# A hybrid encoder trunk: where in memory the two operands of the 256-column products lie to each other

## The chip, the core and the metric

The kernel runs on one NeuronCore of a Trainium2 chip. The metric is the device time of one execution in microseconds (us), median of several runs. The engines are TensorE (PE in the profile; its weight loads are shown apart as PEld), VectorE (DVE), ScalarE (ACT), GpSimd (POOL) and SyncE (SP, which issues most DMAs). A product here is one instruction of TensorE: 128 rows of *moving* data, 128 to 512 columns wide, stream past 128 x 128 *stationary* data, which a weight load has put into the array before.

## The reference

Two layers over 256 tokens of 2048 channels, all float32. Cut to what is computed:

```python
for layer in range(2):
    h = rms_norm(x, norm_mixer_g[layer])
    if layer % 2 == 0:      # convolution module
        a, gate = split(h @ w_pw1 + b_pw1)            # 2048 -> 2 x 2048
        u = a * sigmoid(gate)
        u = depthwise_causal_conv(u, w_dw, width=31) + b_dw
        x = x + silu(layer_norm(u, ln_g, ln_b)) @ w_pw2 + b_pw2
    else:                   # multi-head latent attention, 16 heads, chunk mask
        c_q, c_kv, k_pe = split(h @ w_in, [512, 1024])
        q = rms_norm(c_q, q_norm_g) @ w_q_up          # per head 128 + 64 (rotary)
        kv = rms_norm(c_kv, kv_norm_g) @ w_kv_up      # per head keys 128, values 128
        x = x + attention(q, kv, k_pe) @ w_o
    h = rms_norm(x, norm_mlp_g[layer])
    x = x + square(relu(h @ w1)) @ w2                 # 2048 -> 8192 -> 2048
return rms_norm(x, final_norm_g)
```

## The kernel before

**Products in parts.** To come near float32, every operand is split into a high part, which ScalarE writes as a rounded copy (`hi`, type float32r), and a low part, which VectorE (in the convolution mostly GpSimd) writes as the rest (`lo`). A product of two matrices is then three products of TensorE: high x high, high x low, low x high. `mm3` (L194 to L198) issues the three with the tokens or weights' parts as its caller orders them.

**Stages.** In order of time: the convolution's first product (L858 to L860, about 19 to 208 us) with the depthwise taps on VectorE (L960) under it; layer norm and the second product (L196 to L198, moving weights 512 wide); the first MLP (about 320 to 1010 us); the attention (its input product to 1040 us, queries, keys, values and scores to about 1150, the output product behind); the second MLP.

**The tokens.** The normalised input of a stage lies in four tiles `xt`, which `open_xt` (L316) takes from a pool at the right end of the memory: for each of 16 pieces of 128 channels the high part (256 columns, one for each token) and right behind it the low part. `xh(k)` is a piece's high part, `xl(k)` its low part, `xhl(k)` both in one operand of 512 columns. Before the change one set of `xt` serves the convolution and the first MLP and the attention's input product; a second one is opened for the second MLP.

**The MLP's first product.** Weights w1 come in units of 128 output columns, each in two chunks of 8 pieces. `hi_lo` (L418) makes the two tiles of a chunk; the low tile is longer by `LO_GAP` = 64 floats, and its data begin `at` floats behind its start. In `up_unit` the high weights are stationary against `xhl(k)`, 512 columns (L515), and the low weights against `xh(k)`, 256 columns (L513). A unit's order on TensorE is 8 products of L515, 16 of L513, 8 of L515. MLP units of the second product (512 columns, L196 to L198) stand between them.

**The convolution's first product.** Here the weights are stationary and the tokens move: for each block of 128 channels (16 blocks) there are 16 pieces x 2 halves (value and gate) x 3 products = 96 products of 256 columns: high weights against `xh(k)` (L858) and `xl(k)` (L859), low weights against `xh(k)` (L860). VectorE does most of the 31 taps of each block, into banks of sums which ScalarE starts (L916).

**The attention's products.** Keys (L1420 to L1422) and queries (L1443 to L1445) have weights stationary and the normalised compressed tokens `kvh`, `kvl`, `qh`, `ql` moving, 256 columns. Values and the queries' rotary parts (`mm3`, L196 to L198) have it the other way round: tokens stationary, weights moving, 256 columns. The scores' rotary part (L1525) has `kpA` moving and `qpA` stationary.

**Where things lie.** Pads of a few floats (`PAD_CONST`, `PAD_RIGHT`, `PAD_O` and so on) shift the tiles behind them. *Distance* means in this document: start address of a product's moving operand minus that of its stationary operand, in bytes within a partition, modulo 256. It is worked out from the addresses that the built program gives its tiles. Consecutive pieces lie a multiple of 256 bytes apart, so the distance to the next product's stationary data is the same inside a run of like products.

Of the kernel before, what the change touches and what calls it, by code (L numbers as in the profile page):

```python
# [10 lines left out]
F32 = mybir.dt.float32  # L11
# [7 lines left out]
P = 128  # L19
# [19 lines left out]
PAD_SMALL = 8  # L39
PAD_RIGHT = 40  # L40
LO_GAP = 64
PAD_STATS = 48
PAD_O = 64
WB = 6
LOOK = WB // 2 - 1
LAST_PE = 22
# [37 lines left out]
def trunk_kernel(  # L84
# [55 lines left out]
    def nm(s):  # L140
        uid[0] += 1
        return f"{s}_{uid[0]}"
# [104 lines left out]
    def to_T(src, k0, hi, lo, gain, pt=None):  # L247

        pt = pt if pt is not None else tr_tile()
        for j in range(2):  # L250
            for t in range(T):
                nc.tensor.transpose(  # L252
                    pt[:, j * S + t * P : j * S + (t + 1) * P],
                    src[:, t, (k0 + j) * P : (k0 + j + 1) * P],
                    ident,
                )
        ps = [pt[:, j * S : (j + 1) * S] for j in range(2)]
        for j in range(2):
            hi_part(ps[j], hi(k0 + j), gain[:, k0 + j : k0 + j + 1])
        for j in range(2):  # L260
            lo_part(ps[j], hi(k0 + j), lo(k0 + j), gain[:, k0 + j : k0 + j + 1])
# [46 lines left out]
    def right_pool(name, bufs):  # L308

        xt_cx[0].close()  # L310
        xt_cx[0] = ExitStack()
        return xt_cx[0].enter_context(tc.tile_pool(name=name, bufs=bufs, side="right", reuse_waits="tile"))

    ctx.callback(lambda: xt_cx[0].close())

    def open_xt(name):  # L316
        pool = right_pool(name, 1)
        xt[:] = [
            pool.tile([P, KC // NNB, 2 * S], F32R, name=nm("xt")) for _ in range(NNB)
        ]  # L320

    xhl = lambda k: xt[k // 4][:, k % 4, :]
    xh = lambda k: xhl(k)[:, :S]
    xl = lambda k: xhl(k)[:, S:]
    open_xt("xt0")
    spare = []

    xh_kt = lambda k, t: xh(k)[:, t * P : (t + 1) * P]
# [2 lines left out]
    def residual_stage(last, gain, r_scale=None):  # L331


        ssq = small.tile([P, T, NNB], F32, tag="ssq", name=nm("ssq"), bufs=2) if last else None

        def add(n, ps, t):
            sl = slice(n * NB, (n + 1) * NB)
            if r_scale is None:
                nc.vector.tensor_tensor(xs[:, t, sl], ps[t], xs[:, t, sl], op=ALU.add)
            else:  # L340
                nc.vector.scalar_tensor_tensor(
                    out=xs[:, t, sl], in0=ps[t], scalar=r_scale[:, t : t + 1], in1=xs[:, t, sl],
                    op0=ALU.mult, op1=ALU.add,
                )

        def prepare(n, only=None):
            sl = slice(n * NB, (n + 1) * NB)
            if last:
                if gain is not None:
                    for j in range(2):  # L350
                        to_T(xs, 4 * n + 2 * j, xh, xl, gain)
                for t in range(T) if only is None else [only]:
                    nc.scalar.activation(spare[-1](), xs[:, t, sl], AF.Square, accum_out=ssq[:, t, n : n + 1])

        return ssq, add, prepare
# [63 lines left out]
    def hi_lo(n, at=0):  # L419
        hi = wpool.tile([P, n, NB], F32R, tag="hi", name=nm("hi"), bufs=WB)  # L420
        lo = wpool.tile([P, n * NB + LO_GAP], F32R, tag="lo", name=nm("lo"), bufs=WB)
        return [hi, lo[:, at : at + n * NB].rearrange("p (a b) -> p a b", b=NB)]

    def split_into(parts, src):
        nc.scalar.activation(parts[0], src, AF.Copy)  # L425
        nc.vector.tensor_tensor(parts[1], src, parts[0].bitcast(F32), op=ALU.subtract)  # L426
# [52 lines left out]
    def mlp(layer, ssq, next_gain, finish=None, before=None, last_w1=None):  # L479
# [11 lines left out]
        def up_units(hs, q, p, extra):  # L491

            sevens = SEVENS[layer][q]
            held = {}
            large = p in sevens or (q == PARTS - 1 and p in LATE_G[layer])

            def up_unit(b):
                ps = []

                def chunk(h):  # L500
                    def prep(raw, parts):
                        parts[h] = [a.rearrange("p a (j n) -> p (a j) n", n=P) for a in hi_lo(2, LO_GAP - 8)]
                        split_into(parts[h], raw[:, 8 * h : 8 * h + 8, :])

                    def run(parts):
                        if not ps:
                            ps.append(acc_tile())
                        wh, wl = parts.pop(h)
                        for low in (h, 1 - h):
                            for j in range(8):  # L510
                                k = 8 * h + j
                                if low:
                                    nc.tensor.matmul(ps[0][:, :S], wl[:, j, :], xh(k), start=False, stop=False)  # L513
                                else:
                                    nc.tensor.matmul(ps[0], wh[:, j, :], xhl(k), start=k == 0, stop=k == KC - 1)  # L515

                    def out():
                        if b == 0:
                            held["u"] = u_tile()
                        nc.scalar.activation(held["u"][:, b, :], ps[0], AF.Copy)  # L520

                    if h == 0:
                        return Chunk(prep, run)
                    return Chunk(prep, run, [add, lambda: None, square, forms, part] + extra if b == 1 else [], now=out)

                unit = Unit(rows(w1, 0, KC, ((q * NPAIR + p) * 2 + b) * P, P), KC, [chunk(h) for h in range(2)])
                unit.last_read = 1
                return unit

            def add():  # L530
                v = held["u"][:, :, :S]
                nc.vector.tensor_tensor(v, v, held["u"][:, :, S:], op=ALU.add)

            def square():
                n_s[0] += large
                v = held["u"][:, :, :S]
                nc.scalar.activation(v, v, AF.Relu)
                if p in sevens:
                    held["f"] = f = f_tile()
                    nc.scalar.activation(f[:, 0:4, :].rearrange("p (b t) n -> p b (t n)", b=2), v, AF.Square)  # L540
                    held["src"], shape, tag, n = f[:, 1:8, :], [P, 7, P], "s", N_S
                else:
                    nc.scalar.activation(v, v, AF.Square)
                    held["src"], shape = v, [P, 2, S]
                    tag, n = ("s", N_S) if large else ("g", N_G)
                held["hl"] = [mp.tile(shape, F32R, tag=tag + c, name=nm(tag + c), bufs=n) for c in "hl"]

            def forms():
                if p in sevens:
                    f = held["f"]  # L550
                    nc.vector.tensor_tensor(
                        f[:, 4:6, :], f[:, 0:1, :].broadcast_to([P, 2, P]), f[:, 1:3, :], op=ALU.subtract
                    )
                    nc.vector.tensor_tensor(f[:, 6, :], f[:, 1, :], f[:, 5, :], op=ALU.subtract)
                    nc.vector.tensor_tensor(f[:, 7, :], f[:, 3, :], f[:, 6, :], op=ALU.subtract)

            def part():
                hs[p] = held["hl"]
                split_into(hs[p], held["src"])

            if large:
                blocked[square] = lambda: n_s[0] < N_S and not (p in sevens and sums_left)
            return [up_unit(b) for b in range(2)]
# [235 lines left out]
    with ExitStack() as cx:  # L799
# [21 lines left out]
        sl_ = cv.tile([P, KC, S], F32R, name="sl_")  # L821
        cv.tile([P, PAD_STATS], F32, name="pad_stats")
        stats = cv.tile([P, T, KC // 2, 6], F32, name="stats")
# [201 lines left out]
        with tc.manual_schedule():  # L1025
# [57 lines left out]
            for c in range(1, KC + 1):  # L1083
                n = UC * c
# [84 lines left out]
            for m in range(NP):  # L1169
# [17 lines left out]
                sl = slice(i * NB, (i + 1) * NB)  # L1187
                nc.vector.tensor_tensor(xs[:, t, sl], xs[:, t, sl], b2[:, sl], op=ALU.add)

        ssq, add, prepare = residual_stage(True, g_mlp[0])  # L1190
        for b in range(2):
            for t in range(T):
# [62 lines left out]
    with ExitStack() as cx:  # L1255
        at = cx.enter_context(tc.tile_pool(name="at", bufs=1, reuse_waits="tile"))
# [58 lines left out]
        raws, parts = {}, {}  # L1315
# [28 lines left out]
        def prefetch(n=9):  # L1344
            while pending and n > 0:
# [3 lines left out]
                if h == 1:  # L1349
                    u_load(u + 3)  # L1350

        kvh = at.tile([P, KR // P, S], F32R, name="kvh")
        kvl = at.tile([P, KR // P, S], F32R, name="kvl")
        qh = at.tile([P, QR // P, S], F32R, name="qh")
# [15 lines left out]
        for i in range(2):  # L1370
            for j in range(HG):
                nc.scalar.activation(qpB[i][DR:, j, :], mq[DR:, :], AF.Copy)
        pad_o = at.tile([P, PAD_O], F32, name="pad_o")
        nc.gpsimd.memset(pad_o, 0.0)
# [202 lines left out]
        with tc.manual_schedule():  # L1577
# [9 lines left out]
            for k in range(KC):  # L1587
                u, j = divmod(k, 2)
# [17 lines left out]
            for k in range(KC):  # L1606
                u, j = divmod(k, 4)
# [59 lines left out]
            for g in range(NG):  # L1667
                for i in range(HG):
                    h = g * HG + i

                    n = -(-len(work) // (HG - i))
# [116 lines left out]
```

## Time and profile before

| | |
|---|---|
| Median of 3 runs | 1936.2 us (1936.07 to 1936.22) |
| Profiled execution | 1935.74 us, its span 1933.9 us |
| TensorE's granted clock, mean | 0.999 |
| HBM | 363.68 MB read, 189 GB/s over the span |

The page's groups name a line, an engine, an operation, the tiles (out<-in), the shapes, how many there are, then their busy time in us, the mean duration of one in ns, and idle time of the engine before them. The timeline has start and duration in us. A product's duration (about 0.28 us for 256 columns, 0.39 for 512) is longer than its spacing to the next one, since products overlap in the pipeline; the spacing is read from the starts.

### The profile page before, as it was taken

The numbers are of one execution on the slowest core, as the hardware profiler recorded it, in microseconds if no ns is written. First come the engines' busy times: TensorE is split into PE (matmuls) and PEld (weight loads), VectorE is DVE, ScalarE is ACT, GpSimd is POOL, SyncE is SP. The second block draws the span as 40 slices with busy tenths as digits, with TensorE's granted clock in tenths as the row PEclk, the third lists the DMA queues.
The fourth block names the chain that finished last, engine by engine and source line by source line (L and its number), as shares of the span: only waits on it lengthen the run. The fifth ranks groups of instructions, "written<-read, shape, count | busy, mean of one in ns | idle before, by whom it ended". The sixth has DMA issues, their size and how long they took to land.

```text
span 1933.9 us, 28479 instructions
## 1 busy us (share of the span) xinstructions
PE 1910.2 (99%) x10778; PEld 1676.2 (87%) x10778; DVE 1651.6 (85%) x2374; ACT 1204.9 (62%) x1709; POOL 224.0 (12%) x183
## 2 busy tenths in 40 slices
PE   7999999999999999999999999999999999999998
PEld 7999888888888888888899998888888888888886
DVE  5999875789999999999976665657999999999887
ACT  5556664766666666666566665556766666666654
POOL 5999400000000000000001410000000000000000
PEclk9999999999999999999999999999999999999999
DMA  8666456857666667666646445765667766766663
GB/s 235 185 176 176 141 186 174 220 172 208 197 207 204 205 199 212 202 198 215 198 143 181 123 152 175 198 184 174 203 190 210 214 196 195 214 202 197 211 222 109
DMA packets 407113, 367.62 MB, mean 190 GB/s; under 512 B 15416, under 2 KB 351936, under 8 KB 406720
## 3 DMA queue, kind: packets, MB, share of 16 engines
q1 hardware_dynamic: 405952, 363.63, 63.0%
q10 hardware_dynamic: 1024, 2.17, 0.3%
q8 instruction: 84, 1.38, 0.3%
q14 instruction: 53, 0.43, 0.1%
HBM read 363.68 MB, written 2.10 MB: 189 GB/s over the span
## 4 chain that ended last, share of the span: by engine, by line
PE 98%; DVE 1%; DMA 1%; ACT 0%; issue 0%; DVEq 0%; ACTq 0%
PE acc L515 24%; PE acc L196 15%; PE acc L197 15%; PE acc L198 15%; PE acc L513 12%; PE acc L859 3%; PE acc L858 3%; PE acc L860 3%; PE acc L252 1%; PE sum L908 1%; PE acc L1443 0%; PE acc L1445 0%; PE acc L1444 0%; PE acc L1420 0%; PE acc L1421 0%; PE acc L1422 0%
## 5 line engine op out<-in xcount | busy, mean ns | idle before, releaser
L426 DVE TENSOR_TENSOR lo<-raw,hi 128x1024 fp32r<-128x1024 f32 (+1 forms) x512 | 571.8, 1124 | 88.0 <-ACT hi L425 87.7
L425 ACT ACTIVATE hi<-raw 128x1024 fp32r<-128x1024 f32 (+1 forms) x512 | 480.0, 971 | 66.0 <-PE acc L197 65.8
L515 PE MATMUL acc<-xt,hi 128*128 128x512 f32 x2048 | 504.0, 391 | 0.0
L515 PEld LDWEIGHTS acc<-xt,hi 128*128 128x128 f32 x2048 | 374.9, 188 | 72.6
L196 PE MATMUL acc<-hi,sh 128*128 128x512 f32 x930 | 362.7, 390 | 0.0
L198 PE MATMUL acc<-lo,sh 128*128 128x512 f32 x930 | 361.9, 389 | 0.0
L197 PE MATMUL acc<-hi,sl 128*128 128x512 f32 x802 | 312.0, 389 | 0.0
L513 PEld LDWEIGHTS acc<-xt,lo 128*128 128x128 f32 x2048 | 257.7, 188 | 10.9
L513 PE MATMUL acc<-xt,lo 128*128 128x256 f32 x2048 | 259.8, 279 | 0.0
L170 ACT ACTIVATE hi<-raw 128x1024 fp32r<-128x1024 f32 (+2 forms) x184 | 180.0, 1006 | 47.0 <-PE acc L197 42.9
L198 PEld LDWEIGHTS acc<-lo,sh 128*128 128x128 f32 x930 | 174.6, 188 | 36.3
L196 PEld LDWEIGHTS acc<-hi,sh 128*128 128x128 f32 x930 | 174.6, 188 | 35.9
L171 DVE TENSOR_TENSOR lo<-raw,hi 128x1024 fp32r<-128x1024 f32 (+2 forms) x118 | 132.9, 1147 | 68.6 <-ACT hi L170 63.0
L425 ACT ACTIVATE hi<-V 128x1024 fp32r<-128x1024 f32 x94 | 99.6, 1060 | 130.7 <-DVE V L721 123.6
L197 PEld LDWEIGHTS acc<-hi,sl 128*128 128x128 f32 x802 | 150.6, 188 | 31.1
L960 DVE SCALAR_TENSOR_TENSOR sum<-ub,w_dw,sum 128x256 f32<-128x256 f32 x400 | 163.5, 488 | 8.7 <-ACT sum L916 7.0
L171 POOL TENSOR_TENSOR lo<-raw,hi 128x1024 fp32r<-128x1024 f32 x66 | 157.8, 2413 | 24.5 <-ACT hi L170 24.5
L425 ACT ACTIVATE hi<-T 128x1024 fp32r<-128x1024 f32 x94 | 99.5, 1058 | 92.5 <-DVE T L709 69.0
L858 PE MATMUL acc<-xt,hi 128*128 128x256 f32 x512 | 146.3, 286 | 0.0
L859 PE MATMUL acc<-xt,hi 128*128 128x256 f32 x512 | 145.0, 283 | 0.5 <-DVE xt L209 0.5
L860 PE MATMUL acc<-xt,lo 128*128 128x256 f32 x512 | 144.9, 283 | 0.0
L520 ACT ACTIVATE U<-acc 128x512 f32<-128x512 f32 x128 | 75.8, 592 | 108.7 <-PE acc L515 108.6
(270 smaller groups left out, 2808.9 us busy)
## 6 DMA issues: line engine op xcount, KB each, us to landing
raw<-in_mlp_w SPq DMA_DIRECT2D x256, 1024.0 KB, 6.2
raw<-in_conv_w_pw SPq DMA_DIRECT2D x64, 512.0 KB, 5.6
raw<-in_conv_w_pw SPq DMA_DIRECT2D x16, 1024.0 KB, 5.1
raw<-in_mla_w_o SPq DMA_DIRECT2D x16, 1024.0 KB, 5.3
raw<-in_mla_w_kv_up SPq DMA_DIRECT2D x8, 1024.0 KB, 5.4
raw<-in_mla_w_in SPq DMA_DIRECT2D x8, 576.0 KB, 3.8
raw<-in_mla_w_in SPq DMA_DIRECT2D x4, 1024.0 KB, 7.4
raw<-in_mla_w_q_up SPq DMA_DIRECT2D x16, 256.0 KB, 5.0
```

The lines of the kernel that those rows point to most:

```text
L170: nc.scalar.activation(hi, raw[:, js, :], AF.Copy)
L171: eng.tensor_tensor(lo, raw[:, js, :], hi.bitcast(F32), op=ALU.subtract)
L196: nc.tensor.matmul(ps, sh, mh, start=start, stop=False)
L197: nc.tensor.matmul(ps, sl, mh, start=False, stop=False)
L198: nc.tensor.matmul(ps, sh, ml, start=False, stop=stop)
L425: nc.scalar.activation(parts[0], src, AF.Copy)
L426: nc.vector.tensor_tensor(parts[1], src, parts[0].bitcast(F32), op=ALU.subtract)
L513: nc.tensor.matmul(ps[0][:, :S], wl[:, j, :], xh(k), start=False, stop=False)
L515: nc.tensor.matmul(ps[0], wh[:, j, :], xhl(k), start=k == 0, stop=k == KC - 1)
L858: nc.tensor.matmul(o, wh[:, bs], xh(k), start=k == 0, stop=False)
L859: nc.tensor.matmul(o, wh[:, bs], xl(k), start=False, stop=False)
L860: nc.tensor.matmul(o, wl[:, bs], xh(k), start=False, stop=k == KC - 1)
```

## The change

It moves tiles. No instruction is added, removed or put elsewhere in an engine's order, and the waits are the same; one memset clears a smaller pad.

```diff
-PAD_O = 64
+PAD_XT = 16
+PAD_KV = 48
+PAD_O = 16
...
-    def open_xt(name):
+    def open_xt(name, pad=0):
         pool = right_pool(name, 1)
         xt[:] = [
             pool.tile([P, KC // NNB, 2 * S], F32R, name=nm("xt")) for _ in range(NNB)
         ]
+        if pad:
+            pool.tile([P, pad], F32, name=nm("pad_xt"))
...
-    open_xt("xt0")
+    open_xt("xtc", PAD_XT)
...
-                        parts[h] = [a.rearrange("p a (j n) -> p (a j) n", n=P) for a in hi_lo(2, LO_GAP - 8)]
+                        parts[h] = [a.rearrange("p a (j n) -> p (a j) n", n=P) for a in hi_lo(2, LO_GAP // 4)]
...
+        open_xt("xt0")
         ssq, add, prepare = residual_stage(True, g_mlp[0])
...
+        at.tile([P, PAD_KV], F32, name="pad_kv")
         kvh = at.tile([P, KR // P, S], F32R, name="kvh")
```

- The MLP's low weights begin 64 bytes into their tile, where it was 224.
- The convolution has a set of `xt` of its own, 64 bytes lower than before; the set for the first MLP is opened behind the convolution, at the old addresses.
- `kvh`, `kvl`, `qh`, `ql`, `kpA`, `kpB`, `qpB` lie 192 bytes higher; `PAD_O` is smaller by as much, so what follows (`oh`, `ol`) stays.

| Products (moving columns) | Lines before | Number | Distance before | Distance after |
|---|---|---|---|---|
| MLP, low weights (256) | L513 | 2048 | 32 | 192 |
| Convolution (256) | L858, L859, L860 | 1536 | 0 | 192 |
| Keys and queries (256) | L1420 to L1422, L1443 to L1445 | 384 | 0 | 192 |
| Values, queries' rotary parts (256) | L196 to L198 with `kvh`, `kvl`, `qh`, `ql` | 288 | 0 | 64 |
| Scores, rotary (128 and 256) | L1525 | 32 | 0 | 192 |
| MLP, high weights (512) | L515 | 2048 | 0 | 0 |
| All products of 512 columns by `mm3` | L196 to L198 | the rest | 0 | 0 |
| Attention's input product (288) | L196 to L198 with `xt` | 192 | 0 and 128 | 0 and 128 |

## The prediction

> **What bounds the kernel now.** I read the page first: the busy shares and the chain of waits (its shares by engine and by line).
>
> ```profile
> span 1933.9 us, 28479 instructions
> PE 1910.2 (99%) x10778; PEld 1676.2 (87%) x10778; DVE 1651.6 (85%) x2374; ACT 1204.9 (62%) x1709; POOL 224.0 (12%) x183
> PE 98%; DVE 1%; DMA 1%; ACT 0%; issue 0%; DVEq 0%; ACTq 0%
> ```
>
> The chain is TensorE from end to end, so the time is the sum over products of the spacing from one product's start to the next one's. An edit that moves no instruction can still change that spacing, and this is the only way in which this one can act. A share of the whole says nothing of the stages, so the second view is busy time by stretch (us, then busy us and instructions of PE, PEld, DVE, ACT, POOL, then clock, DMA share, GB/s): the convolution after its start, the first MLP, the attention's queries and keys.
>
> ```profile
> 70.00:208.00 138.00, 138.00 (x1154) 137.99 (x1153) 137.29 (x353) 78.83 (x136) 128.85 (x84) 1.00 0.64 178
> 500.00:600.00 100.00, 100.00 (x512) 85.45 (x511) 96.83 (x113) 68.32 (x84) 0.00 (x0) 1.00 0.67 203
> 1085.00:1150.00 65.00, 64.44 (x529) 63.33 (x529) 46.00 (x111) 41.05 (x106) 19.14 (x28) 1.00 0.43 130
> ```
>
> TensorE never rests and its clock is whole. But in the convolution VectorE is busy for 137.29 of 138.00 us as well: two engines set that stage, while in the MLP VectorE has 3.2 us of 100 to spare and in the attention 19 of 65.
>
> The third view is the timeline of TensorE, for the spacing (first number: start in us). A busy time of 0.39 or 0.28 us is not it, since products overlap in the pipeline. First an MLP stretch:
>
> ```profile
> 564.98 0.39 PE L196 MATMUL acc<-hi,sh 128*128 128x512 f32 x1
> ...
> 569.51 0.39 PE L198 MATMUL acc<-lo,sh 128*128 128x512 f32 x1
> 569.74 1.98 PE L515 MATMUL acc<-xt,hi 128*128 128x512 f32 x8
> 571.56 2.03 PE L513 MATMUL acc<-xt,lo 128*128 128x256 f32 x16
> 573.43 2.00 PE L515 MATMUL acc<-xt,hi 128*128 128x512 f32 x8
> 575.27 0.39 PE L196 MATMUL acc<-hi,sh 128*128 128x512 f32 x1
> ```
>
> From 564.98 to 569.74 stand 21 products of 512 columns: 4.76 / 21 = 226.7 ns each, at distance 0. The 16 products of L513 (256 columns, distance 32) take 573.43 - 571.56 = 1.87 us, 116.9 ns each. The two groups of 8 products of L515 beside them take 1.82 and 1.84 us, where 8 x 226.7 is 1.813: the run of L513 also costs its neighbours 0.034 us. So 16 of them cost 1.87 + 0.034 = 1.904 us, 119.0 ns each. Now 256 columns at distance 0, in the convolution and in the queries, with products of 128 columns behind them, and 288 columns at distances 0 and 128 in turn:
>
> ```profile
> 123.65 0.28 PE L860 MATMUL acc<-xt,lo 128*128 128x256 f32 x1
> ...
> 125.81 0.28 PE L860 MATMUL acc<-xt,lo 128*128 128x256 f32 x1
> ```
>
> ```profile
> 1099.79 0.28 PE L1444 MATMUL acc<-ql,hi 128*128 128x256 f32 x1
> ...
> 1101.47 0.22 PE L196 MATMUL acc<-kTh,qTh 128*128 128x128 f32 x1
> 1101.53 0.28 PE L197 MATMUL acc<-kTh,qTl 128*128 128x128 f32 x1
> ...
> 1101.97 0.34 PE L196 MATMUL acc<-kTh,qTh 128*128 128x256 f32 x1
> ```
>
> ```profile
> 1009.89 0.29 PE L198 MATMUL acc<-lo,xt 128*128 128x288 f32 x1
> ...
> 1012.29 0.29 PE L198 MATMUL acc<-lo,xt 128*128 128x288 f32 x1
> ```
>
> Convolution: 18 products in 2.16 us, 120.0 ns. Queries: 14 in 1.68 us, 120.0 ns. 288 columns: 18 in 2.40 us, 133.3 ns, without a difference between the two distances. 128 columns: 4 in 0.44 us, 110 ns. The three widths lie on one line: (226.7 - 120.0) / 256 = 0.417 ns a column, and 120.0 - 256 x 0.417 = 13.3 ns that every product pays whatever its width. These 13.3 ns are all that an address could save on a product; at distance 32 a product pays 10.2 inside its run, and 12.3 with what its neighbours lose.
>
> **The change part by part.** No engine gets another instruction, order or wait; only the memset of a pad shrinks. What changes is where four sets of tiles lie. The counts:
>
> ```profile
> L513 PE MATMUL acc<-xt,lo 128*128 128x256 f32 x2048 | 259.8, 279 | 0.0
> L858 PE MATMUL acc<-xt,hi 128*128 128x256 f32 x512 | 146.3, 286 | 0.0
> L1420 PE MATMUL acc<-kvh,hi 128*128 128x256 f32 x64 | 18.4, 288 | 0.0
> L196 PE MATMUL acc<-hi,kvh 128*128 128x256 f32 x64 | 18.3, 287 | 0.0
> L196 PE MATMUL acc<-hi,qh 128*128 128x256 f32 x32 | 9.1, 283 | 0.0
> ```
>
> L858 has two sisters (L859, L860): 1536 products. L1420 has two, and so has L1443 with as many: 384. The two rows of L196 have two each (L197, L198): 288, which go to distance 64, since their operands have changed places.
>
> *The spacing at 192.* No row shows it. The good end is streaming alone, 256 x 0.417 = 106.7 ns. A row beside it is the 110 ns of products with half as many columns, which something other than streaming sets. The bad end isn't zero gain: a distance can also cost, as the neighbours of L513 show, which pay up to 27 ns in a group of 8 (1.84 against 1.813), 3.4 ns each; that gives 123.4. The only row at a distance other than 0 or 128 has 116.9, on the good side. I take the middle of 110 and 116.9, 113.4 ns, and the same for 64.
>
> The Trainium skill, "TensorE: Matmul & The Clock Gate", section "Back-to-back issue gap", gives columns / 2.4 + 2.5 ns. Its estimate for 256 columns is 109.2 ns, and for 512 it is 215.8, where the row here has 226.7, so the trace disagrees by some 11 ns. If 192 reached that gap, the MLP would save 20 us, the attention 7, and the time would be 1906.
>
> *MLP.* A run of 16 then takes 16 x 113.4 = 1.814 us, and I leave the neighbours' 0.034 in place, since the L515 beside it stay at distance 0: 1.848 against 1.904, 56 ns. 2048 / 16 = 128 runs: 7.2 us. What could hide it is VectorE, which makes the lower parts: 128 runs in the two MLPs' 1335 us are 9.6 in 100 us, 0.5 us saved where VectorE has 3.2 to spare, so all of it counts. With 106.7 and no loss beside it: 16 x 12.3 = 0.197 us, 25.2 us in all, 1.9 in 100 us, still covered.
>
> *Attention.* 384 + 288 = 672 products x (120.0 - 113.4) = 4.4 us, TensorE alone sets the stage. Good end 672 x 13.3 = 8.9.
>
> *Convolution.* 1536 x 6.6 = 10.1 us on TensorE, but VectorE's taps are the cover that is gone: it can only use what it idles now. These are its idle times there (in brackets: us, and who ended them):
>
> ```profile
> 35.35 1.54 DVE L960 SCALAR_TENSOR_TENSOR sum<-ub,w_dw,sum 128x256 f32<-128x256 f32 x3 [4.50 <-ACT sum L916]
> 46.94 1.27 DVE L960 SCALAR_TENSOR_TENSOR sum<-ub,w_dw,sum 128x256 f32<-128x256 f32 x3 [1.11 <-ACT sum L916]
> 70.18 0.49 DVE L960 SCALAR_TENSOR_TENSOR sum<-ub,w_dw,sum 128x256 f32<-128x256 f32 x1 [1.43 <-ACT sum L916]
> 209.25 0.48 DVE L883 SCALAR_TENSOR_TENSOR ub<-acc,vecs_cv,sg 128x256 f32<-128x256 f32 x1 [1.04 <-ACT sg L880]
> ```
>
> The first tap comes earlier by one block's products, 96 x 6.6 = 0.6 us; the idle 1.11 and 1.43 us can go, as TensorE is 4 blocks or 2.5 us ahead by 70 us: 2.5 in all up to there, then VectorE runs through to 208, where 1.04 more is open. I take 3.0 of 3.6 at most. TensorE then waits for VectorE instead, through the sums' banks and ScalarE.
>
> Sum: 7.2 + 4.4 + 3.0 = 14.6 us. The profiled execution took 1935.74 us (1.8 outside its span), the median is 1936.2, 0.5 above it: **1921.6 us**.
>
> **The rivals.**
> *A. 192 is like 0.* For it: 288 columns at 128 space like those at 0, so perhaps only what lies below a multiple of 64 counts, and 32 gains because it is none. Against: nothing shows 64 or 192. The MLP loses 2048 x (120.0 - 119.0) = 2.0 us, the rest nothing: 1938.2.
> *B. Addresses do not matter.* What separates 116.9 from 120.0 is then the stage, not the distance, and the time stays 1936.2. Against it: clock, widths and full queues are alike in both rows. The Trainium skill, "SBUF — State Buffer", section "Who interferes with whom", says so: moving data and weights have a read port each, and "PE and ACT never wait on anyone"; the 10.2 against 13.3 ns speak against it without settling it.
> *C. 192 is worse than 0.* Weight load and moving data then meet more often than at 0. For it: next to the run at 32, wide products pay 3.4 ns more each, so 13.3 is no ceiling. Against: all rows of 256 columns stand at or under 120. Price at 123.4 ns: MLP 2048 x 4.4 = 9.0, convolution 1536 x 3.4 = 5.2 (TensorE alone sets it again), attention 2.3: 16.5 us, 1952.7. It decides from about 120.4 ns, where the three sums together pass 0.2%.
> *D. VectorE is no cap.* Its taps would have to shorten when TensorE's accesses thin out; the convolution gives 10.1 instead of 3.0: 1914.5. Nothing in the profile speaks for it but the stage's even balance.
>
> **How the numbers follow.** A measurement of this kernel tells about 0.2% from no change, 3.9 us. Forecast 0.55, D 0.05, A 0.11, B 0.04, C 0.25. Faster 0.60, same 0.15 (A and B), slower 0.25. The forecast's own range is 1904 (between the middle value and the good end, 25.2 + 8.9 + 3.6 = 37.7 us, 1898.5) to 1931. A and B reach to 1938.2; half of C is let in, to 1950. So 1904 to 1950.
>
> **What would show it.** A step is right if L513's runs of 16 take about 1.81 us, L1420 to L1445 and L196 to L198 (kvh, qh) space at about 113 ns, and the convolution ends about 3 us earlier with VectorE at 100% and waits of TensorE in it. 120.0 everywhere is A, 1.87 us and 120.0 as before is B, over 120.4 is C, a convolution shorter by 10 us without waits is D. What makes the prediction wrong soonest is the spacing at 192, on which all three terms hang; next a loss of L515 beside the runs larger than 0.034 us.

## The result, and the profile after

The changed kernel takes 1934.21 us (median of 12 runs, 1933.56 to 1934.86), the kernel before, run beside it, 1936.01: 1.8 us less, a ratio of 0.9991 (95% interval 0.9982 to 1.0). By the 0.2% of the prediction that is no change that can be told, where 14.6 us less had been forecast. From here on lines of the changed kernel are given by its own numbers: L517 and L519 are the MLP's low and high products (L513 and L515 before), L862 to L864 the convolution's (L858 to L860), L912 its tap products (L908), L198 to L200 `mm3`.

The page of the changed kernel: span, busy time, shares of the chain of waits, and three groups.

```profile
span 1932.1 us, 28479 instructions
...
PE 1903.0 (98%) x10778; PEld 1669.4 (86%) x10778; DVE 1650.8 (85%) x2374; ACT 1204.7 (62%) x1709; POOL 223.3 (12%) x183
...
PE 88%; DVE 9%; ACT 1%; POOL 1%; issue 0%; DMA 0%; SPq 0%; DVEq 0%; ACTq 0%; POOLq 0%
...
L517 PE MATMUL acc<-xt,lo 128*128 128x256 f32 x2048 | 262.4, 281 | 0.0
L862 PE MATMUL acc<-xt,hi 128*128 128x256 f32 x512 | 143.6, 280 | 0.0
L864 PE MATMUL acc<-xt,lo 128*128 128x256 f32 x512 | 142.2, 278 | 0.6 <-POOL lo L173 0.6
```

Two things stand out. The chain now runs 9% of its way through VectorE: a stage has changed hands, and it is the convolution. And the three groups moved in opposite directions: L862 is busy 2.7 us less than before, L517 2.6 us *more*. The share that each stage has in the 1.8 us is read from TensorE's timeline, by the start of the same instruction in both kernels:

| Marker (us) | Before | After | Shift | The stage since the last marker |
|---|---|---|---|---|
| Last block's tap products | 209.79 | 205.94 | -3.85 | |
| Layer norm's transposes | 224.25 | 222.04 | -2.21 | convolution -2.2 |
| First MLP begins | 320.13 | 317.91 | -2.22 | 0 |
| Attention begins | 991.91 | 990.70 | -1.21 | first MLP +1.0 |
| Second MLP begins | 1253.43 | 1250.74 | -2.69 | attention -1.5 |
| End | 1933.93 | 1932.13 | -1.80 | second MLP +0.9 |

A stage that isn't changed can come out up to 0.3 us longer or shorter in another profiled execution: in e10 below the first MLP, the same as in before, takes 0.3 us more.

The timeline of TensorE in the changed kernel, the stretch of the first MLP that the prediction showed of before (start, duration, then the group):

```profile
568.09 1.97 PE L519 MATMUL acc<-xt,hi 128*128 128x512 f32 x8
569.90 2.05 PE L517 MATMUL acc<-xt,lo 128*128 128x256 f32 x16
...
571.79 2.00 PE L519 MATMUL acc<-xt,hi 128*128 128x512 f32 x8
573.63 0.39 PE L198 MATMUL acc<-hi,sh 128*128 128x512 f32 x1
```

The run of 16 takes 571.79 - 569.90 = 1.89 us, 118.1 ns each, where it was 116.9. The neighbours take 1.81 and 1.84 us, about 0.025 above 16 x 226.7 ns. With them a product costs (1.89 + 0.025) / 16 = 119.7 ns (before: 119.0); over all 128 runs it is 119.6 against 118.8. Distance 192 is worse than 32 here.

Two blocks of the convolution at the same distance, two stretches of the same view:

```profile
107.96 0.28 PE L864 MATMUL acc<-xt,lo 128*128 128x256 f32 x1
...
118.91 0.29 PE L864 MATMUL acc<-xt,lo 128*128 128x256 f32 x1
```

```profile
120.86 0.28 PE L864 MATMUL acc<-xt,lo 128*128 128x256 f32 x1
...
130.04 0.28 PE L864 MATMUL acc<-xt,lo 128*128 128x256 f32 x1
```

93 products in 10.95 us are 117.7 ns each; 81 in 9.18 us are 113.3. So one distance has two spacings. 113.4 was the prediction's value; the MLP has the other one.

The end of the convolution, first in before, then in the changed kernel (in brackets: idle us and who ended it):

```profile
209.79 5.02 PE L908 MATMUL sum<-ub,dg 128*128 128x256 f32 x22 [1.15 <-DVE ub L883]
```

```profile
205.94 6.70 PE L912 MATMUL sum<-ub,dg 128*128 128x256 f32 x22 [4.29 <-DVE ub L887]
```

And the busy times by stretch there, after (the columns of the prediction's second view: PE, PEld, DVE, ACT, POOL, clock, DMA share, GB/s):

```profile
70.00:205.00 135.00, 131.09 (x1139) 130.69 (x1137) 135.00 (x350) 79.14 (x135) 129.32 (x86) 1.00 0.67 185
205.00:207.00 2.00, 1.06 (x5) 0.96 (x6) 2.00 (x8) 1.09 (x3) 0.68 (x2) 0.99 0.03 8
207.00:209.00 2.00, 2.00 (x7) 1.54 (x6) 2.00 (x7) 2.00 (x4) 1.85 (x3) 0.50 0.00 0
```

VectorE is busy for the whole 135.00 us; TensorE, which never rested there before, has 3.9 us to spare, waits 4.29 us at the end for the last block's `ub`, and is then granted half its clock: the same 22 tap products take 6.70 us instead of 5.02.

### The profile page after: what moved, and what is told of

Read it like the earlier page. It is cut to its first block, busy times and chain, and to the rows that moved or that the text cites. A ratio compares the mean times of both kernels' runs of the same rounds, so it can differ in the third digit from the quotient of the medians.

```text
span 1932.1 us, 28479 instructions
## 1 busy us (share of the span) xinstructions
PE 1903.0 (98%) x10778; PEld 1669.4 (86%) x10778; DVE 1650.8 (85%) x2374; ACT 1204.7 (62%) x1709; POOL 223.3 (12%) x183
## 4 chain that ended last, share of the span: by engine, by line
PE 88%; DVE 9%; ACT 1%; POOL 1%; issue 0%; DMA 0%; SPq 0%; DVEq 0%; ACTq 0%; POOLq 0%
PE acc L519 24%; PE acc L198 15%; PE acc L199 15%; PE acc L200 15%; PE acc L517 13%; DVE sum L964 7%; PE acc L254 1%; PE sum L912 1%; DMA xs<-in_x 0%; ACT hi L172 0%; PE acc L863 0%; PE acc L862 0%; PE acc L864 0%; PE acc L1562 0%; PE acc L1426 0%
## 5 line engine op out<-in xcount | busy, mean ns | idle before, releaser
L519 PE MATMUL acc<-xt,hi 128*128 128x512 f32 x2048 | 503.2, 391 | 0.0
L519 PEld LDWEIGHTS acc<-xt,hi 128*128 128x128 f32 x2048 | 376.0, 188 | 72.7 <-ACT hi L429 0.3
L198 PE MATMUL acc<-hi,sh 128*128 128x512 f32 x930 | 362.7, 390 | 0.0
L200 PE MATMUL acc<-lo,sh 128*128 128x512 f32 x930 | 361.9, 389 | 0.0
L517 PEld LDWEIGHTS acc<-xt,lo 128*128 128x128 f32 x2048 | 259.3, 189 | 9.8
L517 PE MATMUL acc<-xt,lo 128*128 128x256 f32 x2048 | 262.4, 281 | 0.0
L200 PEld LDWEIGHTS acc<-lo,sh 128*128 128x128 f32 x930 | 174.6, 188 | 36.3
L198 PEld LDWEIGHTS acc<-hi,sh 128*128 128x128 f32 x930 | 174.6, 188 | 35.9
L862 PE MATMUL acc<-xt,hi 128*128 128x256 f32 x512 | 143.6, 280 | 0.0
L863 PE MATMUL acc<-xt,hi 128*128 128x256 f32 x512 | 142.2, 278 | 1.0 <-DVE xt L211 1.0
L864 PE MATMUL acc<-xt,lo 128*128 128x256 f32 x512 | 142.2, 278 | 0.6 <-POOL lo L173 0.6
```

What stands on the lines that cost most here:

```text
L198: nc.tensor.matmul(ps, sh, mh, start=start, stop=False)
L200: nc.tensor.matmul(ps, sh, ml, start=False, stop=stop)
L862: nc.tensor.matmul(o, wh[:, bs], xh(k), start=k == 0, stop=False)
L863: nc.tensor.matmul(o, wh[:, bs], xl(k), start=False, stop=False)
```

## The experiments

Two theories were tested first. *D* (not the rival D of the prediction): a distance has one spacing, and 192 was simply mis-sized. *S*: at one distance there are several steady spacings, and what runs before a product decides which one it gets. For the convolution the question was whether VectorE is the cap and what the lost 1.7 us are.

### The three parts alone (e3, e4, e5)

Only the convolution (the change with the other two undone), only the MLP, only the attention (both: before, with that part):

```diff
 # e3_conv_only, against the changed kernel
-PAD_O = 16
+PAD_O = 64
-    ... hi_lo(2, LO_GAP // 4)
+    ... hi_lo(2, LO_GAP - 8)
-        at.tile([P, PAD_KV], F32, name="pad_kv")
 # e4_mlp_only, against before
-    ... hi_lo(2, LO_GAP - 8)
+    ... hi_lo(2, LO_GAP // 4)
 # e5_att_only, against before
-PAD_O = 64
+PAD_O = 16
+PAD_KV = 48
+        at.tile([P, PAD_KV], F32, name="pad_kv")
```

> Only the convolution's tokens in a pool of their own at distance 192; MLP at 32, attention at 0 as before. If the parts of the change simply add, by the stages of the two profiles: the convolution's start of the taps to its end 2.2 us earlier, the rest unchanged, so 1933.8 us. Rival: the convolution's head start is lost again behind it (the second product or the MLP waits for weights instead), then 1936.0.

> Only the MLP's low weights at distance 192 instead of 32. If the parts add: two MLPs at about 0.9 us more each, 1937.9 us, runs of 16 at 117.8 ns a product inside and some 27 ns lost by the products beside them. Rival: the MLP's loss in the changed kernel comes from its other start time against the DMAs and not from the distance; then 1936.0.

> Only the attention's tiles moved (keys and queries at 192, values and rotary queries at 64). If the parts add: the stretch from the first key product to the last one 1.4 us shorter, 1934.6 us, with keys and queries at 113.5 or 117.8 ns and the values at 117.6. Rival: the attention's gain needs the earlier start; then 1936.0.

The kernel before took 1935.85 us beside them: convolution alone 1934.32 (ratio 0.9992, 0.9983 to 1.0001), MLP alone 1937.43 (1.0008, 0.9999 to 1.0017), attention alone 1934.54 (0.9993, 0.9984 to 1.0002). Singly, none can be told from no change; the sum -1.5 + 1.6 - 1.3 = -1.2 is near the -1.8 of the whole. MLP alone moves both MLPs by +0.86 and +0.87 us, as in the stage table. In the profiled execution of the convolution alone the loss at the end is larger:

```profile
206.59 7.67 PE L912 MATMUL sum<-ub,dg 128*128 128x256 f32 x22 [3.82 <-DVE ub L887]
```

3.20 us are won up to that row, 2.65 go into its longer duration (7.67 against 5.02), 0.6 remain. This execution took 1935.12 us; the eleven of this kernel range from 1933.31 to 1935.65, while those of before range from 1935.67 to 1936.07. So the loss differs from one execution to the next; why, no run shows.

### All distances in the MLP (e2)

The two chunks of a run are given each of the 64 distances in steps of 4 bytes, one distance a run, in both MLPs.

```diff
+                place = (q * NPAIR + p) * 2 + b
-    ... hi_lo(2, LO_GAP // 4)
+    ... hi_lo(2, place)
```

> The changed kernel, but each of the 128 MLP units (128 output columns of w1) puts its low weights at another offset, 0 to 63 floats in turn, so that one run shows the spacing of the 256-column products of the MLP's low weights at all 64 distances in steps of 4 bytes, twice (once in each layer). If the distance alone sets the spacing (theory D), a unit at 192 has 117.8 ns as in the changed kernel, one at 32 has 116.6, one at 0 has 120.0, and the curve between is smooth or repeats with 16, 32 or 64 bytes; both layers agree within 0.3 ns. If the way into a run sets which of several steady spacings it falls into (theory S), the curve jumps between a few values such as 113.3, 116.7, 117.8 and 120.0, and the same distance may give different values in the two layers. Either way the edit adds nothing else: the time lies between 1930 and 1945 us.

One profile holds all (1936.32 us, before 1935.85). TensorE's timeline for the best distance, 180, and the worst, 52 (L518 and L520 are the low and the high products in this kernel and the next):

```profile
451.42 1.99 PE L518 MATMUL acc<-xt,lo 128*128 128x256 f32 x16
453.25 1.09 PE L520 MATMUL acc<-xt,hi 128*128 128x512 f32 x4
```

```profile
804.55 2.13 PE L518 MATMUL acc<-xt,lo 128*128 128x256 f32 x16
806.51 1.32 PE L520 MATMUL acc<-xt,hi 128*128 128x512 f32 x5
```

The runs take 1.83 and 1.96 us. From the starts of products inside a run, in ns (second: with what the neighbours lose, per product):

| Distance | 0 | 32 | 52 | 64 | 76 | 128 | 168 | 176 | 180 | 184 | 192 |
|---|---|---|---|---|---|---|---|---|---|---|---|
| Spacing | 119.5 | 116.6 | 122.8 | 117.8 | 114.2 | 120.2 | 114.6 | 118.4 | 114.2 | 118.4 | 117.9 |
| With neighbours | 121.2 | 118.8 | 125.0 | 121.0 | 115.8 | 121.2 | 116.2 | 122.3 | 115.8 | 121.4 | 119.6 |

At these distances both MLPs agree to 0.1 or 0.2 ns, so this is no noise. Only 0, the first unit of each MLP, differs: 119.5 ns (shown) in the first, 118.6 in the second. But 4 bytes more change the spacing by 4 ns, so a value taken from the rows of other distances, as the prediction's was, has nothing to rest on. Between D and S this run does not decide: the curve is not smooth, as D had it, but the layers agree, and what runs ahead of a run is alike in nearly all units.

### Two halves of a run at distances of their own (e1)

```diff
+                place = (q * NPAIR + p) * 2 + b
-    ... hi_lo(2, LO_GAP // 4)
+    ... hi_lo(2, 8 * (place % 8 if h == 0 else place // 8))
```

> The changed kernel, but the two halves of a run of 16 low-weight products of the MLP lie at distances of their own: the first 8 products at one of 0, 32, 64, ... 224, the last 8 at one of them, all 64 pairs, each once in each layer. Theory S (a run falls into a steady spacing that its way in decides): the last 8 products at 192 have different means behind different first halves, some at 113.3 and some at 117.8 ns. Theory D (distance alone): the last 8 at 192 have 117.8 within 0.5 ns after the first two products, whatever the first half was, and the last 8 at 32 have 116.7. Time 1930 to 1945 us by both.

One execution, 1935.97 us (before 1935.96).

The second 8 products of a run stand at 192 in all four of these rows, from the 9th product on; the first 8 stood at 32, 64, 0 and 192 (TensorE's timeline, each with the next row):

```profile
489.00 1.07 PE L518 MATMUL acc<-xt,lo 128*128 128x256 f32 x8
489.91 0.40 PE L520 MATMUL acc<-xt,hi 128*128 128x512 f32 x1
```

```profile
483.50 1.07 PE L518 MATMUL acc<-xt,lo 128*128 128x256 f32 x8
484.41 0.40 PE L520 MATMUL acc<-xt,hi 128*128 128x512 f32 x1
```

```profile
416.32 1.11 PE L518 MATMUL acc<-xt,lo 128*128 128x256 f32 x8
417.26 0.40 PE L520 MATMUL acc<-xt,hi 128*128 128x512 f32 x1
```

```profile
436.89 1.11 PE L518 MATMUL acc<-xt,lo 128*128 128x256 f32 x8
437.84 0.40 PE L520 MATMUL acc<-xt,hi 128*128 128x512 f32 x1
```

0.91 us behind 32 and 64, 0.94 and 0.95 behind 0 and 192: inside these halves, away from the edges, 113.4 and 117.8 ns. Eight products at the same distance have two spacings, and what differs ahead of them is the distance of the first half; so D falls and S holds. These four rows do not all use the same weight buffer; e8 below rules the buffer out. Behind 0 and 192 the second half has 117.8; behind each of the other six it ends at 113 to 114 ns, behind 96 only after four uneven products (120, 114, 124, 118 ns). Distance 64 likewise has 113.4 behind first halves at 0 and 32, and about 118 behind the others. With neighbours a product of the pair 32, 192 costs 117.1 ns, of 32 throughout 118.7 in this kernel, of 192 throughout 119.6.

### The 512-column products (e6)

They make up most of TensorE's time. Here the high tile is shifted instead of the low one, also the moving one of `mm3`, over all 64 distances.

```diff
-    def hi_lo(n, at=0):
+    def hi_lo(n, at=None):
+        if at is None:
+            turn_hl[0] += 1
+            at = turn_hl[0] % 64
-        hi = wpool.tile([P, n, NB], ...)
-        lo = wpool.tile([P, n * NB + LO_GAP], ...)
-        return [hi, lo[:, at : at + n * NB]...]
+        hi = wpool.tile([P, n * NB + LO_GAP], ...)
+        lo = wpool.tile([P, n, NB], ...)
+        return [hi[:, at : at + n * NB]..., lo]
...
+                place = (q * NPAIR + p) * 2 + b
-    ... hi_lo(2, LO_GAP // 4)
+    ... hi_lo(2, place)
```

> The gap moves from the MLP's low tiles to its high tiles: low weights all at distance 0, and the high weights of unit n (stationary against 512 columns) begin n floats into their tile, n = 0 to 63; the high parts of the second product's weights (moving, 512 columns) shift by 0 to 63 floats in turn. One run shows the spacing of 512-column products at 64 distances. If the 32 cycles that a 512-column product pays above its columns at distance 0 (226.7 against 213.3 ns) come from the meeting of the two reads (theory S or D alike), the spacing spreads between some 220 and 236 ns and single distances lie below 226.7. Rival: 512-column products hide the weight load whole at any distance but pay a fixed 13.3 ns, and the spacing is 226.7 at each. Time by the first 1925 to 1960 us, by the second 1938 to 1942, since the low weights' products then pay 120 to 121 ns.

1960.27 us (before 1935.96). At the distances other than 0 the means run from 227.9 to 235.6 ns for the MLP's high products and from 228.2 to 237.3 for `mm3`: distances matter here as well, and no mean is below the 226.7 of distance 0 in the kernel before, where the expectation had some. Nothing was found to gain there.

### The MLP with better distances (e7, e8)

180 for both halves, and 32 with 192 behind it; both against before:

```diff
 # e7_mlp_180
-    ... hi_lo(2, LO_GAP - 8)
+    ... hi_lo(2, 19)
 # e8_mlp_32_192
-    ... hi_lo(2, LO_GAP - 8)
+    ... hi_lo(2, LO_GAP // 4 if h else LO_GAP - 8)
```

> The kernel before, with the MLP's low weights at distance 180 instead of 32 (offset 19 floats). The fine sweep had 115.8 ns a product there with the neighbours' loss, and 118.8 at 32. If the distance and the way in (always products of 512 columns at distance 0) fix the steady spacing (theory S), all 128 runs take it: 2048 x 3.0 ns = 6.1 us, 1929.8 us. Rival: the sweep's single units at 180 owed it to the units at other distances beside them; then some runs have 117 to 118 ns and the time is 1933 or more.

> The kernel before, with the first 8 low-weight products of a run at 32 as they were and the last 8 at 192. Theory S: behind a first half at 32 the products at 192 settle at 113.4 ns (the pairs run had 117.1 a product over the run with the neighbours' loss, against 118.7 to 118.8): 2048 x 1.6 = 3.4 us, 1932.5 us, although a whole run at 192 made the kernel slower. Theory D (192 costs the MLP 117.8 whatever is ahead): half of the loss of the MLP part alone, 1936.7.

1929.86 us against 1935.74 (0.9969, 0.9957 to 0.9982) and 1932.39 (0.9983, 0.9974 to 0.9991). The run of before's 571.56, at 180:

```profile
568.59 1.97 PE L515 MATMUL acc<-xt,hi 128*128 128x512 f32 x8
570.40 1.99 PE L513 MATMUL acc<-xt,lo 128*128 128x256 f32 x16
572.23 2.00 PE L515 MATMUL acc<-xt,hi 128*128 128x512 f32 x8
```

1.83 us. (118.8 - 115.8) x 2048 = 6.1 us were worked out from the table of distances, 5.9 came: once a distance's cost in its own surroundings is measured, the sum over products predicts the time. The pair gives 3.4 us, where D would have it lose. Its second halves have 113.2 to 113.7 ns in all 128 runs (10th to 16th product); in the MLP alone (e4), where they lie at the same addresses and only the first halves differ, all 128 have 117.5 to 118.0. So the products ahead decide, and not the buffer.

### Is VectorE the convolution's cap? (e10, e11)

The last two taps of 15 of the 16 blocks are left out, in before and in the convolution alone; VectorE has less to do, and the sums lack these taps.

```diff
-            left[c] = list(range(w + n, W))
+            left[c] = list(range(w + n, W if c == KC - 1 else W - 2))
```

> The kernel before, which leaves out the last two of the 31 taps of each convolution block but the last: 30 of VectorE's instructions of 0.4 us, 12 us. If TensorE sets this stage before the change, the last block's tap products still begin at about 209 us and the time falls by less than 1 us: 1935 to 1936. Rival (VectorE set it already): up to 10 us less.

> The convolution part alone, with the same two taps of each block but the last left out. If VectorE's taps are the cap on what the faster products bring (the prediction's step), TensorE's whole gain comes out now: 1536 x some 5 ns = 7.8 us, the last block's tap products begin at about 202 us instead of 206, and the time is some 5 us under the kernel before with the same taps left out. Rival (GpSimd's low parts, busy 129 of 135 us, hold it): they begin at about 205 to 206 as with all taps, and the time is 1 to 2 us under that kernel.

In before: 1935.89 us against 1935.91 (1.0, 0.999 to 1.001), nothing. With the convolution's products at 192: 1928.63 (0.9963, 0.9948 to 0.9977). The tap products then stand so:

```profile
202.58 5.02 PE L912 MATMUL sum<-ub,dg 128*128 128x256 f32 x22 [1.14 <-DVE ub L887]
```

209.79 - 202.58 = 7.2 us earlier, a wait as short as before's, and 5.02 us. So TensorE was the cap before, VectorE is it after, and the products alone would have given 7.2 us. GpSimd, busy for 129.32 of the 135.00 us above and just as long here, did not hold them back.

### The clock at the end of the convolution (e9)

38 transposes of the identity, whose results go nowhere, fill TensorE's wait; against the convolution alone.

```diff
+                if c == KC:
+                    keep_warm(ident, 38)
```

> The convolution part alone, with 38 transposes of the identity (some 4.1 us of TensorE) put into the 4.6 us in which TensorE waits for VectorE ahead of the last block's tap products. In the changed kernel these 22 products then take 6.70 us under a granted clock of 0.50, against 5.02 before. If the clock is what the convolution loses at its end, it comes back: 1.7 us under the 1934.3 of the convolution part alone, 1932.6. Rival: VectorE's last taps set the end anyway, and the clock does not matter: 1934.3.

1931.71 us against 1935.74 before (0.998, 0.9971 to 0.9989), 2.6 under the 1934.32 of the convolution alone; the highest of its eleven executions, 1932.45, is below the lowest of those. TensorE's timeline:

```profile
201.35 4.31 PE L237 MATMUL acc<-ident 128*128 128x128 f32 x38
205.79 5.02 PE L912 MATMUL sum<-ub,dg 128*128 128x256 f32 x22
```

And the busy times of the 6.5 us from there on, first of the convolution alone, then with the transposes (the column behind POOL's is the clock):

```profile
206.00:212.50 6.50, 5.91 (x15) 4.78 (x16) 6.35 (x18) 3.60 (x6) 5.50 (x6) 0.54 0.01 3
```

```profile
206.00:212.50 6.50, 6.50 (x32) 5.68 (x32) 6.50 (x18) 3.38 (x6) 5.59 (x5) 1.00 0.02 3
```

The wait itself stays; what it cost besides was the clock, 0.54 against 1.00. The Trainium skill, "TensorE: Matmul & The Clock Gate", section "What's actually happening", says that the array's clock is halved when an activity window of some 3.4 us finds it idle; idle 3.82 and 4.29 us here went with a clock of 0.50 to 0.54, idle 1.15 us in before left the 5.02 us that the taps also take at 1.00, so the rows agree.

### Everything together (e12)

The changed kernel with the MLP at 180 and the 38 transposes.

```diff
-    ... hi_lo(2, LO_GAP // 4)
+    ... hi_lo(2, 19)
...
+                if c == KC:
+                    keep_warm(ident, 38)
```

> The changed kernel with the MLP at 180 instead of 192 and the 38 transposes ahead of the last block's tap products. If the parts add: convolution -1.5, warm clock -1.7 at most, attention -1.3, MLP -6.1: 1925.3 us, or 1927.0 if the transposes bring nothing. Rival: VectorE caps the MLP too (its 3.2 us idle of 100), then the MLP brings less and the time stays over 1928.

```profile
span 1922.6 us, 28555 instructions
...
PE 1898.0 (99%) x10816; PEld 1664.6 (87%) x10816; DVE 1648.8 (86%) x2374; ACT 1204.3 (63%) x1709; POOL 223.4 (12%) x183
```

1924.49 us against 1935.91 (0.9942, 0.9928 to 0.9955): 11.4 us, of which the convolution has 4.2, the two MLPs 5.9 (2.96 and 2.99 by their stages), the attention 1.2. It beats both kernels.

## Why the prediction was wrong

**What bounds the kernel** held: TensorE from end to end, VectorE next to it in the convolution (e10, e11) and not in the MLP (e7). In the attention a wait for VectorE counted too, as told below.

**The failed step is the spacing at 192.** "I take the middle of 110 and 116.9, 113.4 ns, and the same for 64" took the spacing for a property of the distance. 113.4 does occur, but as one of two steady spacings; 117.8 is the other, and the products ahead decide (e1, e8). That the middle of a row of 128 columns and a row at distance 32 hit one of them to the tenth was luck: the spacing goes up and down by some 4 ns every few bytes (e2), so neither row said anything of 192. The measured 1934.2 us is above the forecast's own range, 1904 to 1931.

| Term | Predicted | Measured | Missed |
|---|---|---|---|
| MLP | -7.2 us | +1.9 | 9.1 |
| Attention | -4.4 | -1.5 | 2.9 |
| Convolution | -3.0 | -2.2 | 0.8 |
| Sum | -14.6 | -1.8 | 12.8 |

**MLP.** All 128 runs are entered from 512-column products at distance 0, and all got 117.8 to 117.9, with 26 ns lost by the neighbours of a run (34 had been left in place, nearly right): 119.6 against 118.8 ns, 2048 x 0.8 = 1.6 us, and 1.58 is what the MLP alone cost. That the sum over products is the time here, with VectorE covered, e7 shows.

**Attention.** Its queries at 192 (TensorE's timeline, first and last of 81 products in 9.18 us) reached 113.3 ns:

```profile
1056.53 0.28 PE L1451 MATMUL acc<-qh,lo 128*128 128x256 f32 x1
...
1065.71 0.28 PE L1451 MATMUL acc<-qh,lo 128*128 128x256 f32 x1
```

Other runs of keys and queries got 117.8; their mean is about 115. Most products at 64 got 117.7 to 117.9, as here, 6 in 0.71 us; three runs of 12 that stand right behind keys or queries at 113.3 to 113.8 got 113.4 themselves. The rows of the first kind:

```profile
1055.46 0.28 PE L200 MATMUL acc<-lo,qh 128*128 128x256 f32 x1
...
1056.17 0.28 PE L200 MATMUL acc<-lo,qh 128*128 128x256 f32 x1
```

"TensorE alone sets the stage" was too strong as well: the 672 products became 2.5 us shorter in sum, but one wait for VectorE's `pr` grew from 0.4 to 1.2 us, and a stop of 0.26 us is new between two transposes of `pr`:

```profile
1084.61 0.70 PE L1553 MATMUL acc<-ident,pr 128*128 128x128 f32 x3 [1.22 <-DVE pr L1547]
```

**Convolution.** The mechanism was right: VectorE runs through, TensorE waits. Its size was 3.9 us rather than 3.0 at the last block's taps. VectorE's idle times that the prediction listed fell from 4.50, 1.11, 1.43 and 1.04 us to 4.37, 0.67, 0.39 and none, 2.65 us in all; where the other 1.2 come from isn't resolved. What the prediction had not asked is what a wait of 4.3 us does to the clock: 1.7 us were given back there (2.6 in the convolution alone), and e9 got them back. On TensorE the products saved 7.2 us (e11) instead of 10.1; about 1.7 of the difference is that every third block (starts 73.9, 107.6, 141.4, 175.2 us) runs at 117.7 and not 113.3: 4 x 96 products x 4.4 ns.

**The rivals.** A (192 like 0) falls: 113.3 to 118 against 119.5 to 120.0. C (192 worse than 0) falls for the same reason, though against 32 it is right: its place, the MLP, was the place that lost. D of the prediction (VectorE no cap) falls by e11. B falls by e2 and e7: the address alone moves the spacing of the same products in the same stage from 114.2 to 122.8 ns. The Trainium skill's sentence in "SBUF — State Buffer", section "Who interferes with whom", that TensorE never waits on anyone, is about engines that share ports; it does not bear B out, since here the start addresses of TensorE's own two operands move its spacing by these 8.6 ns.

**What stays open.** Why a difference of addresses selects a spacing, and why a run keeps the one that it enters with, isn't shown; that both operands' reads meet in the memory is only a guess. Why every third convolution block gets the dear one is open as well: six weight buffers with four used per block repeat every third block, which fits, but no run moved a buffer, and in the MLP, where six buffers take turns as well, all 128 runs agree. The shorter wait of the two at the convolution's end (3.82 us against 4.29) had the longer taps behind it (7.67 us against 6.70); that isn't explained either. A better placement for the attention wasn't tried.

## What to carry to other kernels

A cost that depends on addresses can't be read off one neighbouring row: measure it in the place where it is to apply, with the same instructions ahead of it, best with many placements in one profiled run. Then multiply by the count; that sum came within 0.3 us of the measured time (e7). And where a faster engine will wait for another, ask how long the wait is and what it does to the clock: here a wait of about 4 us cost 1.7 to 2.65 us more behind it, and products of no use in it paid.

## What the hardware showed that was not expected

- The same products at the same distance have two steady spacings, 113.4 and 117.8 ns (256 columns, at 192), chosen by what ran before, and held for runs of 8 to some 90 products.
- 4 bytes of displacement change 256-column products by up to 4 ns (180: 114.2; 176 and 184: 118.4), the same in both layers.
- 512-column products stand at 226.7 ns at distance 0, and at 227.9 to 237.3 on average at the other distances tried (e6).
- After 3.8 to 4.3 us without a product TensorE's granted clock is 0.50 to 0.54 for some us; 22 tap products then take 6.70 to 7.67 us instead of 5.02. With 38 transposes in the wait it stays at 1.00.
